# Pooling mixer rewritten as two TensorE products, and a new order of products in the FFN blocks

## The chip, the cores and the metric

The kernel runs on one core of a Trainium2 chip. The metric is the device time of one launch in microseconds (us). A core has TensorE (PE, with its weight loads listed apart as PEld), VectorE (DVE), ScalarE (ACT), GpSimd (POOL) and SyncE (SP); SP and POOL issue the transfers between the chip's memory and the on-chip memory.

## What is computed

Two layers over 512 tokens of 1024 channels, all float32. Each is: half a SwiGLU feed-forward step (FFN), a mixer, another half FFN step; layer 0's mixer pools, layer 1's convolves. The part that changes most is the pooling mixer:

```python
def pool_mixer(x, w_pool, b_pool, scale):
    # for each group g of 256 channels, window w in (2, 4, 8, 16):
    #   pooled[t] = mean of x[t - w/2 : t + w/2], cut at both ends, minus x[t]
    y = jnp.einsum('bsgc,gcd->bsgd', pooled, w_pool).reshape(B, S, D) + b_pool
    return y * scale
x = x + pool_mixer(rmsnorm(x, norm_g[0, 1]), pool_w[0], pool_b[0], pool_scale[0])
```

A norm's per-token factor r, and the pooling over tokens, commute with the product over channels, so each may be taken on either side of it.

## The kernel before, in words

The residual stream `x` lies on chip as 8 chunks of 128 channels x 512 tokens. Weights arrive as a list of numbered pieces (`pieces`, line 104), up to 128 x 1024, in the order in which they are used. A piece lands in one of 8 `raw` buffers, ACT rounds it to `whi` (line 178), DVE takes the remainder `wlo` (line 185), and a product is three matmuls, hi x hi, hi x lo, lo x hi (`passes`, line 199; lines 200 to 202). `whi` and `wlo` have 4 buffers each. `Norm.add` (line 214) makes the same pair `xh`, `xl` of a chunk of x and its square `sq`, which POOL adds up; `sums` reduces over channels with short matmuls and gives r; `spread` broadcasts r.

An FFN (`ffn`, line 332) has "heads" (4 PSUM banks, one 12-matmul group for each of the 8 chunks), then two phases of blocks (2 and 3 of them), each followed by the output product `ps_o` of 8 chunks in two parts (288 matmuls in phase 2). A block is seven products of 24 matmuls of 512 columns, of Strassen's kind, in the order of `STEPS` (line 39): b11, t1, b21, t2, t3, b22, t4, each with two weight pieces (called first and second piece below). Pieces of t1, t2, t4 are sums: POOL issues a transfer that adds a second matrix onto the raw buffer of an earlier piece of the chain b11, t1, t2, t4, as soon as that one has been converted (lines 168, 189). The s-operands (`sxh`, `sxl`) are sums of quarters of x, made by `Norm.pair` (line 241). A block's hidden values are transposed on PE (`ps_t`) and turned into `hh`, `hl` (lines 348, 350) during the next block, or within the output product behind the last block.

`pool_mixer` (line 479): 48 matmuls give the group product `ps_z`, channels on partitions. Then, chunk after chunk: DVE multiplies by r (line 500), ACT and POOL subtract the identity part from x (lines 503, 504), DVE and POOL form window sums by shifted additions or a running sum (lines 517 to 532), and DVE scales the edges and adds into x (lines 539 to 542); then the next norm's `add`. The heads of the next FFN wait for those chunks.

The order on each engine comes from a scheduler that simulates the program ahead of time; within a manual region the order written is kept.

Of the kernel before, what the change touches and what calls it, by code (L numbers as in the profile page):

```python
# [15 lines left out]
P = 128  # L16
# [8 lines left out]
WINDOWS = (2, 4, 8, 16)  # L25
HEAD = 6
# [12 lines left out]
STEPS = ("b11", "t1", "b21", "t2", "t3", "b22", "t4")  # L39
# [3 lines left out]
EDGE = 8  # L43
# [11 lines left out]
SPLIT_SUMS = ("g02",)  # L55
# [5 lines left out]
    ("dw", NC * KW), ("edge", len(WINDOWS) * 2 * EDGE),  # L61
# [10 lines left out]
def encoder(ctx: ExitStack, tc: tile.TileContext, xT, winh, win, wout, poolw, pw1, pw2h, pw2, vecs, out):  # L72
# [15 lines left out]
    for pool in (const, dpool):  # L88
        nc.vector.memset(pool.tile([P, 16], F32, name="pad"), 0.0)
    npbs = const.tile([P, NC], F32, name="npbs")  # L90
    pscw = const.tile([P, NC], F32, name="pscw")
# [25 lines left out]
    in_chunks = {(l, i): paired if (l, i) == (1, 0) else list(range(NC)) for l in range(2) for i in range(2)}  # L117
# [214 lines left out]
    def ffn(l, i, norm, nxt, pre=None):  # L332
# [19 lines left out]
        def gated_heads():  # L352
            for j in range(FH):
# [9 lines left out]
                two(j, u)  # L363

# [42 lines left out]
        def block(b, todo, first):  # L407
# [5 lines left out]
            product("b11", b, "a11", A, True, False, norm.spread if first else None)  # L413
# [65 lines left out]
    def pool_mixer(norm, nxt):  # L479
        pss = []  # L480
        with tc.manual_schedule(engines={mybir.EngineType.PE}):
            for c in range(NC):
                g, h = divmod(c, 2)
                if c % 4 == 0:
                    wh, wl = piece(("pw", g // 2))
                ps = psum.tile([P, S], F32, tag="mm", name="ps_z")
                for k in range(2):
                    o = ((g % 2) * 2 + k) * 256 + h * P
                    passes(ps, wh[:, o:o + P], wl[:, o:o + P], norm.hi[2 * g + k], norm.lo[2 * g + k], k == 0, k == 1)
                pss.append(ps)  # L490
                if c == 2:
                    norm.sums()
                if c == 4:
                    norm.spread()
        zs, wins = [], []

        def evacuate(c):
            if c < NC:
                zs.append(hpool.tile([P, S], F32, tag="h", name="z"))
                nc.vector.tensor_tensor(out=zs[c], in0=pss[c], in1=norm.rb, op=ALU.mult)  # L500

                u = hpool.tile([P, S], F32, tag="h", name="u")
                nc.scalar.activation(u, zs[c], AF.Identity, scale=vec("psc", c), bias=npbs[:, c:c + 1])
                nc.gpsimd.tensor_tensor(out=x[c], in0=x[c], in1=u, op=ALU.subtract)

        def window(c):

            if c >= NC:
                return
            w = WINDOWS[c // 2]  # L510
            b = w // 2
            z = zs[c]
            win = hpool.tile([P, S], F32, tag="h", name="win")
            wins.append(win)
            add = nc.vector if c in ADD_ON_VECTOR else nc.gpsimd
            if w == 2:
                add.tensor_copy(out=win[:, 0:1], in_=z[:, 0:1])
                add.tensor_tensor(out=win[:, 1:], in0=z[:, 1:], in1=z[:, :S - 1], op=ALU.add)
            elif w == 4:
                two = wpool.tile([P, D], F32, tag="raw", name="two", bufs=RAWS)  # L520
                add.tensor_copy(out=two[:, 0:1], in_=z[:, 0:1])
                add.tensor_copy(out=two[:, S:S + 1], in_=z[:, S - 1:S])
                add.tensor_tensor(out=two[:, 1:S], in0=z[:, 1:], in1=z[:, :S - 1], op=ALU.add)
                add.tensor_copy(out=win[:, 0:1], in_=two[:, 1:2])
                add.tensor_tensor(out=win[:, 1:], in0=two[:, 2:S + 1], in1=two[:, :S - 1], op=ALU.add)
            else:

                run = wpool.tile([P, D], F32, tag="raw", name="run", bufs=RAWS)
                nc.gpsimd.memset(run[:, 0:b + 1], 0.0)
                nc.vector.tensor_tensor_scan(out=run[:, b + 1:b + 1 + S], data0=ones_c.to_broadcast([P, S]), data1=z, initial=0.0, op0=ALU.mult, op1=ALU.add)  # L530
                nc.vector.tensor_copy(out=run[:, b + 1 + S:S + 2 * b], in_=run[:, b + S:b + S + 1].to_broadcast([P, b - 1]))
                nc.vector.tensor_tensor(out=win, in0=run[:, w:S + w], in1=run[:, :S], op=ALU.subtract)

        def mix(c):
            w = WINDOWS[c // 2]
            b = w // 2
            win = wins[c]
            e = vec("edge", (c // 2) * 2 * EDGE, 2 * EDGE)
            nc.vector.tensor_tensor(out=win[:, :b], in0=win[:, :b], in1=e[:, :b], op=ALU.mult)
# [497 lines left out]
```

## Time and profile before

| what | value |
|---|---|
| time, median of 3 runs | 1694.42 us (1693.49 to 1694.85) |
| the profiled execution | 1690.47 us, span 1688.6 us |
| PE busy | 1619.0 us, 96% of the span |
| granted TensorE clock, mean | 0.98 of full speed |
| moved | 241.62 MB, mean 143 GB/s |

In the profile a row gives an engine, the line of the kernel, the operation and `out<-in` by the program's names. Matmuls follow each other pipelined: their records overlap, so the distance of two starts is what one costs. The row `[2.75 <-ACT xh L223]` says that the engine stood idle for 2.75 us and what ended it.

### The profile page before, as it was taken

What the parts mean: (1) busy time and instruction counts of PE and PEld (TensorE: products, weight loads), DVE (VectorE), ACT (ScalarE), POOL (GpSimd) and SP (SyncE); (2) the same over time, 40 slices, a digit from 0 to 9 for tenths busy, and PEclk for the clock granted to TensorE, in tenths of its full rate; (3) what the DMA queues carried; (4) which work ended last, traced back from release to release, by engine and by line L of the source; (5) the groups of instructions that cost most, each with busy time, mean ns of one, the idle gap of its engine ahead of it and who ended that gap; (6) DMA issues with size and microseconds to landing.
All of it is one profiled execution on the core that took longest, in us unless ns stands there. A gap on an engine that the chain in (4) does not pass through costs nothing.

```text
span 1688.6 us, 19576 instructions
## 1 busy us (share of the span) xinstructions
PE 1619.0 (96%) x7244; PEld 1328.6 (79%) x7244; DVE 1105.2 (65%) x1411; ACT 786.3 (47%) x1138; POOL 379.5 (22%) x343
## 2 busy tenths in 40 slices
PE   8999999997899999999999999999999999999997
PEld 6788888875688887888788778887777888887785
DVE  8783677449875476665673667439987878367742
ACT  6442445334542344454432444478944645244431
POOL 5100110136110111012101110129982310011111
PEclk9999999998899999999999999999998999999998
DMA  8865886306583888327847886322102586588721
GB/s 255 198 147 151 194 208 167 93 20 162 144 171 117 195 193 186 124 84 176 195 118 170 192 199 162 114 64 66 47 10 75 151 199 144 150 191 206 169 63 50
DMA packets 75839, 241.62 MB, mean 143 GB/s; under 512 B 8544, under 2 KB 8672, under 8 KB 75744
## 3 DMA queue, kind: packets, MB, share of 16 engines
q1 hardware_dynamic: 52704, 156.48, 28.4%
q0 software_dynamic: 23040, 83.90, 28.1%
q8 instruction: 56, 0.92, 0.2%
q14 instruction: 39, 0.32, 0.1%
HBM read 238.25 MB, written 2.10 MB: 142 GB/s over the span
## 4 chain that ended last, share of the span: by engine, by line
PE 61%; DMA 14%; DVE 11%; issue 6%; ACT 5%; POOL 2%; POOLq 0%; DVEq 0%; ACTq 0%; SPq 0%
DMA raw<-win 14%; PE ps_o L202 9%; PE ps_o L200 9%; PE ps_o L201 9%; PE ps_a L200 4%; PE ps_a L202 4%; PE ps_a L201 4%; DVE wlo L185 4%; PE ps_c L201 3%; PE ps_c L200 3%; PE ps_c L202 3%; ACT whi L178 2%; PE ps_t L404 1%; ACT diag L612 1%; PE ps_b L201 1%
## 5 line engine op out<-in xcount | busy, mean ns | idle before, releaser
L185 DVE TENSOR_TENSOR wlo<-raw,whi 128x1024 fp32r<-128x1024 f32 (+2 forms) x468 | 521.0, 1117 | 429.1 <-ACT whi L178 424.1
L178 ACT CAST whi<-raw 128x1024 fp32r<-128x1024 f32 (+2 forms) x468 | 439.4, 944 | 700.6 <-DMA raw<-win 193.4
L168 POOL DMA_DIRECT2D raw<-win x160 | 141.4, 889 | 876.8 <-DMA raw<-win 405.3
L201 PE MATMUL ps_o<-hl,whi 128*128 128x512 f32 x704 | 273.6, 390 | 0.0
L202 PE MATMUL ps_o<-hh,wlo 128*128 128x512 f32 x704 | 273.5, 389 | 0.0
L200 PE MATMUL ps_o<-hh,whi 128*128 128x512 f32 x704 | 273.4, 390 | 0.0
L200 PE MATMUL ps_a<-whi,xh 128*128 128x512 f32 x480 | 189.2, 397 | 0.0
L202 PE MATMUL ps_a<-whi,xl 128*128 128x512 f32 x480 | 189.2, 395 | 0.0
L201 PE MATMUL ps_a<-wlo,xh 128*128 128x512 f32 x480 | 188.4, 393 | 0.0
L235 POOL TENSOR_TENSOR sq<-sq 128x512 f32<-128x512 f32 x47 | 76.1, 1619 | 355.1 <-ACT sq L230 354.6
L202 PEld LDWEIGHTS ps_o<-hh,wlo 128*128 128x128 f32 x704 | 132.2, 188 | 27.3
L201 PEld LDWEIGHTS ps_o<-hl,whi 128*128 128x128 f32 x704 | 132.2, 188 | 27.3
L200 PEld LDWEIGHTS ps_o<-hh,whi 128*128 128x128 f32 x704 | 132.1, 188 | 27.2
L200 PE MATMUL ps_c<-whi,sxh 128*128 128x512 f32 x320 | 125.8, 397 | 0.1
L201 PE MATMUL ps_c<-wlo,sxh 128*128 128x512 f32 x320 | 124.8, 390 | 0.5 <-DVE wlo L185 0.5
L202 PE MATMUL ps_c<-whi,sxl 128*128 128x512 f32 x320 | 124.8, 390 | 0.0
L642 POOL TENSOR_TENSOR part<-part,tap 128x509 f32<-128x509 f32 (+6 forms) x78 | 114.3, 1465 | 25.0 <-ACT tap L641 19.4
L200 PEld LDWEIGHTS ps_a<-whi,xh 128*128 128x128 f32 x480 | 91.7, 191 | 19.5
L202 PEld LDWEIGHTS ps_a<-whi,xl 128*128 128x128 f32 x480 | 90.8, 189 | 19.9
L201 PEld LDWEIGHTS ps_a<-wlo,xh 128*128 128x128 f32 x480 | 91.3, 190 | 19.0
L470 DVE SCALAR_TENSOR_TENSOR x<-ps_o,x 128x512 f32<-128x512 f32 x64 | 44.2, 691 | 63.7 <-PE ps_o L202 63.7
L201 PE MATMUL ps_b<-wlo,sxh 128*128 128x512 f32 x160 | 66.3, 414 | 10.2 <-DVE wlo L185 10.1
(174 smaller groups left out, 2591.2 us busy)
## 6 DMA issues: line engine op xcount, KB each, us to landing
raw<-win SPq DMA_DIRECT2D x160, 512.0 KB, 4.9
raw<-win POOLq DMA_DIRECT2D x160, 512.0 KB, 6.4
raw<-wout SPq DMA_DIRECT2D x64, 256.0 KB, 2.7
raw<-wout SPq DMA_DIRECT2D x32, 512.0 KB, 3.6
raw<-wout SPq DMA_DIRECT2D x32, 384.0 KB, 3.1
raw<-pw SPq DMA_DIRECT2D x18, 512.0 KB, 3.5
raw<-winh SPq DMA_DIRECT2D x32, 256.0 KB, 2.6
raw<-pw2h SPq DMA_DIRECT2D x8, 384.0 KB, 2.9
```

The lines of the kernel that those rows point to most:

```text
L168: nc.gpsimd.dma_start(out=t[:, :w], in_=more, accum_op=ALU.add)
L178: nc.scalar.copy(out=his[n][:, :w], in_=raws[n][:, :w])
L185: nc.vector.tensor_tensor(out=lo[:, :w], in0=raws[n][:, :w], in1=his[n][:, :w].bitcast(F32), op=ALU.subtract)
L200: nc.tensor.matmul(ps, whi, mhi, start=start, stop=False, skip_group_check=True)
L201: nc.tensor.matmul(ps, whi, mlo, start=False, stop=False, skip_group_check=True)
L202: nc.tensor.matmul(ps, wlo, mhi, start=False, stop=stop, skip_group_check=True)
L235: nc.gpsimd.tensor_tensor(out=self.acc, in0=self.acc, in1=sq, op=ALU.add)
L404: nc.tensor.transpose(ps[:, t * P:(t + 1) * P], ht[t][:, c * P:(c + 1) * P], ident)
L470: nc.vector.scalar_tensor_tensor(out=x[c], in0=pss[m], scalar=0.5, in1=x[c], op0=ALU.mult, op1=ALU.add)
L612: nc.scalar.activation(self.diags[-1][:, n % 2, q], ident, AF.Copy, scale=self.wtap[q][:, col:col + 1].bitcast(F32))
L642: nc.gpsimd.tensor_tensor(out=self.part[:, o], in0=self.part[:, o], in1=t[:, o], op=ALU.add)
```

## The change

1. The pooling mixer. The group product now has tokens on the output's partitions (x chunks stationary, 256 columns of the weights moving): 96 matmuls of 256 columns. ACT and DVE scale by r while they split the result into `zh` and `zl`. The pooling, the subtraction of the identity and the edges are a second product, with constant band matrices over tokens as moving operand (`window`): for each of 8 chunks one matmul of 512 columns, seven of 130 to 144, and for six chunks two more of 2 to 8 columns. Each DVE instruction then adds a chunk into x. `x += bias * scale` goes to ACT, ahead of it.
2. The bands: 8 transfers of 128 x 512 (256 KB) and 8 casts on ACT, called just ahead of the output product of phase 2 of FFN (0,0).
3. All blocks: the order of pieces is b11, b21, t1, t2, t3, b22, t4, and b11 and b21 finish one bank before the other is begun (`product_by_pair`).
4. FFN (0,1) takes its heads in the order 0, 4, 1, 5, ..., and the norm ahead of the mixer adds its last square on PE.

```diff
-STEPS = ("b11", "t1", "b21", "t2", "t3", "b22", "t4")
+STEPS = ("b11", "b21", "t1", "t2", "t3", "b22", "t4")
-SPLIT_SUMS = ("g02",)
+SPLIT_SUMS = ("g01", "g02")
...
+        def product_by_pair(step, b, quarter, banks, start, stop, between=None):
+            ws = [piece((step, l, i, b, 0)), piece((step, l, i, b, 1), AHEAD - 1)]
+            for p in range(2):
+                for k in range(KH):
+                    hi, lo = ws[k // 2]
+                    cs = slice((k % 2) * BW, (k % 2 + 1) * BW)
+                    passes(banks[p], *norm.quarter(quarter, k, p), hi[:, cs], lo[:, cs], start and k == 0, stop and k == KH - 1)
+                if p == 0 and between:
+                    between()
...
             A = pair_of_banks("ps_a")
-            product("b11", b, "a11", A, True, False, norm.spread if first else None)
+            product_by_pair("b11", b, "a11", A, True, False, norm.spread if first else None)
...
+            next_()
+            product_by_pair("b21", b, "a12", A, False, True)
+            m1 = [silu(A[p], p) for p in range(2)]
             B = pair_of_banks("ps_b")
             product("t1", b, "s1", B, True, True)
-            next_()
-            product("b21", b, "a12", A, False, True)
-            m1 = [silu(A[p], p) for p in range(2)]
...
+            if ph and last:
+                last()
             for n, (m, h) in enumerate(OUT_ORDER):
...
+    def load_bands():
+        tiles = []
+        for g in range(len(WINDOWS)):
+            two_ = []
+            for q in range(2):
+                raw = hpool.tile([P, S], F32, tag="h", name="band")
+                nc.sync.dma_start(out=raw, in_=bands[g, q])
+                two_.append(hpool.tile([P, S], F32R, tag="h", name="bandr"))
+                nc.scalar.copy(out=two_[q], in_=raw)
+            tiles.append(two_)
+        return tiles
...
+        def mixed(g):
+            gp, j = g % 2, g // 2
+            cs = slice(j * 256, j * 256 + 256)
+            for t in range(NT):
+                if j == 0:
+                    pz[gp][t] = psum.tile([P, S], F32, tag="mm", name="ps_z")
+                ts = slice(t * P, (t + 1) * P)
+                for k in range(2):
+                    wh, wl = w[g // 2]
+                    o = ((g % 2) * 2 + k) * 256
+                    c = 2 * g + k
+                    passes(pz[gp][t][:, cs], norm.hi[c][:, ts], norm.lo[c][:, ts], wh[:, o:o + 256], wl[:, o:o + 256], k == 0, k == 1)
+        def evacuate(gp):
+            for t in range(NT):
+                rt = norm.r[:, t:t + 1]
+                zh[gp][t] = hpool.tile([P, S], F32R, tag="h", name="zh")
+                nc.scalar.activation(zh[gp][t], pz[gp][t], AF.Copy, scale=rt)
+                zl[gp][t] = hpool.tile([P, S], F32R, tag="h", name="zl")
+                nc.vector.scalar_tensor_tensor(out=zl[gp][t], in0=pz[gp][t], scalar=rt, in1=zh[gp][t].bitcast(F32), op0=ALU.mult, op1=ALU.subtract)
+        def window(c):
...
+            for t in range(NT):
+                h_, l_ = zh[gp][t], zl[gp][t]
+                if t == 0:
+                    mm(slice(0, S), h_, first, True)
+                    mm(slice(0, P + e), l_, first[:, :P + e])
+                    if b > 1:
+                        mm(slice(0, b), h_, rest[:, BANDS[2]:BANDS[2] + b])
+                    continue
+                o = slice(t * P - e, min(S, (t + 1) * P + e))
+                at = BANDS[t == NT - 1]
+                m = rest[:, at:at + o.stop - o.start]
+                mm(o, h_, m)
+                if t == NT - 1 and b > 1:
+                    mm(slice(S - b, S), h_, rest[:, BANDS[3]:BANDS[3] + b])
+                mm(o, l_, m, False, t == NT - 1)
...
         with tc.manual_schedule(engines={mybir.EngineType.PE}):
+            w = [piece(("pw", 0)), piece(("pw", 1), AHEAD - 1)]
+            mixed(0)
+            norm.sums()
             for c in range(NC):
+                nc.scalar.activation(x[c], x[c], AF.Identity, bias=psb[:, c:c + 1])
+            mixed(2)
+            evacuate(0)
+            mixed(1)
+            for n, c in enumerate(in_chunks[0, 1]):
+                ps = window(c)
+                if n == 0:
+                    mixed(3)
+                    evacuate(1)
+                nc.vector.scalar_tensor_tensor(out=x[c], in0=ps, scalar=vec("psc", c), in1=x[c], op0=ALU.mult, op1=ALU.add)
+                nxt.add(c)
```

The order of instructions moves at three places that matter below. First PE in the pooling mixer, where the change puts the first chunk's window product between the third and the fourth of the four group products (`bandr` are the bands, `zh` and `zl` the split group product; the bank is `ps_w`):

```order
L202 MATMUL ps_z<-whi_2920,xl_2768 128x256
L540 MATMUL ps_w<-bandr,zh 128x512
L540 MATMUL ps_w<-bandr,zl 128x130
L540 MATMUL ps_w<-bandr,zh 128x132
L540 MATMUL ps_w<-bandr,zl 128x132
L540 MATMUL ps_w<-bandr,zh 128x130
L540 MATMUL ps_w<-bandr,zl 128x130
L200 MATMUL ps_z<-whi_2947,xh_2937 128x256
```

All eight window products and all of `ps_z` now stand ahead of the first head matmul; before, the heads followed `ps_z` directly and waited for DVE, ACT and POOL.

Second ACT in the output product of phase 2 of FFN (0,0). Before (`whi_2578` is the piece of the third chunk's second part, `whi_2608` that of the fourth chunk's first part):

```order
L178 CAST whi_2511<-raw_2509 128x512
L178 CAST whi_2578<-raw_2576 128x512
L348 CAST hh<-ps_t 128x512 x4
L178 CAST whi_2608<-raw_2606 128x1024
L178 CAST whi_2633<-raw_2631 128x512
```

Here the last block's four `hh` casts come directly behind the third chunk's second part. On the same engine at the same place with the change (`whi_2641` is now the fourth chunk's first part):

```order
L178 CAST whi_2544<-raw_2542 128x512
L502 CAST bandr<-band 128x512 x2
L178 CAST whi_2611<-raw_2609 128x512
L502 CAST bandr<-band 128x512 x3
L178 CAST whi_2641<-raw_2639 128x1024
L502 CAST bandr<-band 128x512 x3
L348 CAST hh<-ps_t 128x512 x4
L178 CAST whi_2666<-raw_2664 128x512
```

The four `hh` casts of the last block moved behind the fourth chunk's `whi` and behind the band casts.

Third PE in a block of phase 2 (`whi290` and `whi291` are t1's pieces before; with the change `whi292` and `whi293` are t1's, `whi290` and `whi291` b21's). Before, behind b11:

```order
L202 MATMUL ps_a_7606<-whi289_7555,xl3_5994 128x512
L200 MATMUL ps_b_7646<-whi290_7572,sxh_5701 128x512
L201 MATMUL ps_b_7646<-wlo290_7574,sxh_5701 128x512
...
L200 MATMUL ps_b_7646<-whi291_7607,sxh_5934 128x512
L200 MATMUL ps_b_7647<-whi291_7607,sxh_5934 128x512
...
L201 MATMUL ps_b_7646<-wlo291_7609,sxh_5934 128x512
...
L200 MATMUL ps_a_7605<-whi292_7626,xh4_5684 128x512
```

Here both pieces of t1 follow b11, and b21 comes behind them. With the change, on PE behind b11 of the same block:

```order
L202 MATMUL ps_a_7704<-whi289_7652,xl3_6091 128x512
...
L200 MATMUL ps_b_7790<-whi292_7748,sxh_5798 128x512
L200 MATMUL ps_b_7791<-whi292_7748,sxh_5798 128x512
...
L201 MATMUL ps_b_7790<-wlo292_7750,sxh_5798 128x512
...
L200 MATMUL ps_b_7790<-whi293_7753,sxh_6031 128x512
L200 MATMUL ps_b_7791<-whi293_7753,sxh_6031 128x512
L200 MATMUL ps_a_7703<-whi290_7671,xh4_5781 128x512
```

In this block, and in 11 others of the 20, t1's first piece still stands right behind b11, and b21 now stands between the first and the rest of the second piece; in the other eight, b21 goes ahead of nearly all of t1.

## Rows read from the trace of the kernel before

**Rows 1.** The page, part 1: busy time, share of the span, instructions

```profile
PE 1619.0 (96%) x7244; PEld 1328.6 (79%) x7244; DVE 1105.2 (65%) x1411; ACT 786.3 (47%) x1138; POOL 379.5 (22%) x343
```

**Rows 2.** Busy time of PE, PEld, DVE, ACT, POOL (count) by stretch; then clock, DMA share, GB/s

```profile
361.60:460.00 98.40, 75.66 (x301) 58.81 (x300) 82.31 (x118) 49.91 (x72) 40.30 (x39) 0.86 0.49 123
...
373.60:423.00 49.40, 34.19 (x127) 25.86 (x125) 45.90 (x62) 22.97 (x35) 32.20 (x32) 0.86 0.55 142
...
889.00:1010.00 121.00, 118.18 (x525) 96.60 (x524) 67.52 (x79) 45.60 (x54) 18.33 (x21) 1.00 0.79 187
```

**Rows 3.** Waits: us in total, times, longest; PE over the run, ACT from 330 to 450

```profile
PE ps_h L200 <- ACT xh L223: 11.1, 3, 7.9
PE ps_b L201 <- DVE wlo L185: 10.1, 13, 0.9
PE ps_b L200 <- ACT sxh L255: 6.7, 3, 3.5
...
ACT xh L223 <- DVE x L542: 15.6, 7, 3.8
```

**Rows 4.** PE in order of time, 361 to 451: start, duration, instruction, idle before

```profile
361.70 0.39 PE L200 MATMUL ps_z<-xh,whi 128*128 128x512 f32 x1
...
365.55 0.39 PE L202 MATMUL ps_z<-xh,wlo 128*128 128x512 f32 x1
...
377.37 0.73 PE L200 MATMUL ps_h<-xh,whi 128*128 128x512 f32 x2 [2.75 <-ACT xh L223]
...
382.06 0.63 PE L200 MATMUL ps_h<-xh,whi 128*128 128x512 f32 x1
382.48 0.61 PE L201 MATMUL ps_h<-xl,whi 128*128 128x512 f32 x1
...
397.10 2.07 PE L200 MATMUL ps_h<-xh,whi 128*128 128x512 f32 x4 [7.86 <-ACT xh L223]
...
429.45 0.50 PE L200 MATMUL ps_b<-whi,sxh 128*128 128x512 f32 x1 [3.53 <-ACT sxh L255]
...
450.30 0.61 PE L200 MATMUL ps_c<-whi,sxh 128*128 128x512 f32 x2
```

**Rows 5.** PE in order of time: the short matmuls in the mixer, and what follows

```profile
365.78 0.95 PE L288 MATMUL ps_sum<-ones_c,sq 128*128 128x1 f32 x8
...
366.58 0.49 PE L200 MATMUL ps_z<-xh,whi 128*128 128x512 f32 x1
...
369.45 1.05 PE L299 MATMUL ps_b<-ident,r 128*128 128x128 f32 x8
...
370.26 0.48 PE L200 MATMUL ps_z<-xh,whi 128*128 128x512 f32 x1
```

**Rows 6.** ACT and PE in order of time, output product of FFN (0,0), phase 2

```profile
306.14 2.06 ACT L348 CAST hh<-ps_t 128x512 fp32r<-128x512 f32 x4
312.75 1.05 ACT L178 CAST whi<-raw 128x1024 fp32r<-128x1024 f32 x1 [4.56 <-issue]
...
312.51 0.39 PE L202 MATMUL ps_o<-hh,wlo 128*128 128x512 f32 x1
```

**Rows 7.** POOL, ACT, PE in order of time, one block: t1's first piece, then t2's

```profile
953.03 0.88 POOL L168 DMA_DIRECT2D raw<-win  x1 [1.92 <-DVE wlo L185]
...
962.15 1.05 ACT L178 CAST whi<-raw 128x1024 fp32r<-128x1024 f32 x1 [8.07 <-DMA raw<-win]
...
964.51 0.50 PE L201 MATMUL ps_b<-wlo,sxh 128*128 128x512 f32 x1 [0.42 <-DVE wlo L185]
...
964.86 0.86 POOL L168 DMA_DIRECT2D raw<-win  x1 [7.32 <-DMA raw<-win]
...
970.55 1.06 ACT L178 CAST whi<-raw 128x1024 fp32r<-128x1024 f32 x1
```

**Rows 8.** PE in order of time: two waits in first blocks of other FFNs

```profile
44.38 0.50 PE L200 MATMUL ps_b<-whi,sxh 128*128 128x512 f32 x1 [2.69 <-ACT whi L178]
...
788.41 1.16 PE L299 MATMUL ps_b<-ident,r 128*128 128x128 f32 x8 [1.02 <-POOL r L294]
```

More of the change, by code (lines that the diff above doesn't have):

```diff
@@ L42 @@
 AHEAD = 4
-EDGE = 8
 RMS_EPS = 1e-6
@@ L60 @@
     ("pb", NC), ("psc", NC), ("ba", NC), ("bg", NC), ("bdw", NC), ("lng", NC), ("lnb", NC), ("b2", NC),
-    ("dw", NC * KW), ("edge", len(WINDOWS) * 2 * EDGE),
+    ("dw", NC * KW),
 )
@@ L71, in encoder @@
 @with_exitstack
-def encoder(ctx: ExitStack, tc: tile.TileContext, xT, winh, win, wout, poolw, pw1, pw2h, pw2, vecs, out):
+def encoder(ctx: ExitStack, tc: tile.TileContext, xT, winh, win, wout, poolw, bands, pw1, pw2h, pw2, vecs, out):
     nc = tc.nc
@@ L86, in encoder @@
     mhalf = const.tile([P, NT], F32, name="mhalf")
[L88 to L91, printed above, removed]
+    for pool, n in ((const, 88), (dpool, 16)):
+        nc.vector.memset(pool.tile([P, n], F32, name="pad"), 0.0)
+    psb = const.tile([P, NC], F32, name="psb")
     shift_w = const.tile([P, P], F32R, name="shift_w")
@@ L330, in head_tiles, with ffn @@
         return pss
-    def ffn(l, i, norm, nxt, pre=None):
+    def ffn(l, i, norm, nxt, pre=None, last=None):
         hh, hl = {}, {}
@@ new lines, in pool_mixer @@
+    def pool_mixer(norm, nxt, band):
+        gps = ((0, 2), (1, 3))
+        pz = [[None] * NT for _ in gps]
+        zh, zl = ([[None] * NT for _ in gps] for _ in range(2))
+        def mixed(g):
[18 more added lines that the diff above has]
+        def window(c):
+            g, h = divmod(c, 2)
+            gp, j = g % 2, g // 2
+            zs = slice(j * 256 + h * P, j * 256 + (h + 1) * P)
+            b = WINDOWS[g] // 2
+            e = max(b, 2)
+            first, rest = band[g]
+            ps = psum.tile([P, S], F32, tag="mm", name="ps_w")
+            mm = lambda o, z, m, start=False, stop=False: nc.tensor.matmul(ps[:, o], z[:, zs], m, start=start, stop=stop, skip_group_check=True)
+            for t in range(NT):
[13 more added lines that the diff above has]
+                mm(o, l_, m, False, t == NT - 1)
+            return ps
@@ L490, in pool_mixer @@
[L490 to L539, printed above, removed]
-            if b > 1:
-                nc.vector.tensor_tensor(out=win[:, S - b:], in0=win[:, S - b:], in1=e[:, 2 * EDGE - b:], op=ALU.mult)
-            nc.vector.scalar_tensor_tensor(out=x[c], in0=win, scalar=pscw[:, c:c + 1], in1=x[c], op0=ALU.mult, op1=ALU.add)
-            nxt.add_hi(c)
@@ L545, in pool_mixer @@
-        with ExitStack():
-            for c in range(2):
-                evacuate(c)
-                window(c)
-            for c in range(NC):
-                mix(c)
-                evacuate(c + 2)
-                window(c + 2)
-                nxt.add_lo(c)
+                nc.scalar.activation(x[c], x[c], AF.Identity, bias=psb[:, c:c + 1])
[9 more added lines that the diff above has]
+                nxt.add(c)
@@ L980, in encoder, with window_bands @@
         nc.sync.dma_start(out=out[c * P:(c + 1) * P, :], in_=o)
-def edge_factors():
-    e = np.ones((len(WINDOWS), 2 * EDGE), np.float32)
+def window_bands():
+    out = np.zeros((len(WINDOWS), 2, P, S), np.float32)
     for g, w in enumerate(WINDOWS):
         b = w // 2
-        for t in range(b):
-            e[g, t] = w / (t + b)
-            e[g, 2 * EDGE - b + t] = w / (w - t)
-    return np.broadcast_to(e.reshape(1, -1), (P, e.size))
+        e = max(b, 2)
+        t = np.arange(S)
+        lo, hi = np.clip(t - b, 0, S), np.clip(t + b, 0, S)
+        full = ((t[:, None] >= lo) & (t[:, None] < hi)) / (hi - lo) - np.eye(S)
+        short = np.ascontiguousarray(full.astype(np.float32))
+        short = (short.view(np.uint32) & np.uint32(0xFFFFE000)).view(np.float32)
+        rest = (full - short).astype(np.float32)
+        out[g, 0] = short[:P]
+        m = slice(P - e, 2 * P + e)
+        out[g, 1, :, BANDS[0]:BANDS[0] + P + 2 * e] = short[P:2 * P, m]
+        out[g, 1, :, BANDS[1]:BANDS[1] + P + e] = short[S - P:, S - P - e:]
+        out[g, 1, :, BANDS[2]:BANDS[2] + b] = rest[:P, :b]
+        out[g, 1, :, BANDS[3]:BANDS[3] + b] = rest[S - P:, S - b:]
+    return out
 def columns(v):
@@ L1011 @@
           "bdw": conv_b_dw, "lng": conv_ln_g, "lnb": conv_ln_b, "b2": conv_b_pw2}
-    cols = [columns(v[n]) for n, _ in VECS[:-2]]
+    cols = [columns(v[n]) for n, _ in VECS[:-1]]
     dw = np.asarray(conv_w_dw)[0].reshape(KW, NC, P).transpose(2, 1, 0).reshape(P, NC * KW)
```

24 lines of the change are left out of this document (8 added, 16 removed).

## The prediction

> **What bounds the kernel now.** I read the page first, then the stretches, then the waits, then the instructions in order of time. The page says that PE is busy 96% of the span [rows 1]; a table by stretch shows where the other 4% lies. In the blocks of FFN (1,0) PE is busy 118.2 of 121.0 us at full clock, but between 361.6 and 460 only 75.7 of 98.4 us, at a mean clock of 0.86 [rows 2]. That second stretch is the pooling mixer, the heads of FFN (0,1) and its first block. PE waits longest there for `xh` (11.1 us) and for `sxh` (6.7 us), and ACT, which makes `xh`, waited 15.6 us for DVE's last step on a chunk of x [rows 3]. So PE waits for the shifted additions on DVE and POOL; DVE is busy 45.9 of the 49.4 us from 373.6 to 423 [rows 2].
>
> A matmul of 512 columns costs 0.227 us: from 361.70 to 365.55 there are 17 steps [rows 4]. That is the 2.4 GHz level. Behind idle times the steps are 0.42 us (382.06 to 382.48, rows 4), the 1.2 GHz level.
>
> The stretch from the first `ps_z` (361.70) to the first matmul of t2 (450.30) takes 88.6 us [rows 4]. Its work at full clock is 48 matmuls of `ps_z`, 96 of the heads and 72 of b11, t1 and b21, 216 x 0.227 = 49.0 us, and some 40 short ones at 0.10 us: the eight of `ps_sum` take 0.80 us from 365.78 to 366.58, the eight of `ps_b` 0.81 us [rows 5]. So 53 us are work and 35 us are waits and low clock. This is what can be won.
>
> **The mixer's stretch with the change.** The same stretch ends at t2's first matmul, with the same three products done. Its PE work:
> - `ps_z`: 96 matmuls of 256 columns. The trace has none of this width. Half of 0.227 is the lower end (0.114), 0.227 the upper. I take 0.12, since records of 128 columns and of 1 column cost 0.10 alike [rows 5], so a weight load does not hold it above that: 11.5 us (10.9 to 21.8).
> - Windows: 8 matmuls of 512 columns (1.8 us), 12 of 2 to 8 columns at 0.10 (1.2 us), and 56 of 130 to 144 columns. For these the nearest row is `ps_b`, 128 columns: four products are written there as eight records, so a product costs 0.20 us and a record 0.10 [rows 5]. These bound the price from both sides; I take 0.21, a whole product with its columns scaled up, because nothing in the trace shows a short product in one record: 11.8 us (5.6 to 12.7). Together 14.8 us.
> - Heads 96 x 0.227 = 21.8, sums and broadcast 32 short ones 3.3, b11, t1 and b21 72 x 0.227 = 16.3.
>
> The sum is 67.7 us. What waits remain? The first window needs r and four evacuations. They run on ACT and DVE beside the two group products that follow the sums (5.8 us); an evacuation costs DVE what its average instruction costs in this stretch, 45.9 / 62 = 0.74 us [rows 2], four are 3 us and r about 2. The second four have three window products as cover. A chunk then needs one DVE add, `xh` and `xl`, some 1.5 us of DVE, against 1.9 us of its window on PE, and the heads begin only behind all windows, so `xh` is ready each time. The pairs for `sxh` have the heads, b11 and most of b21 as cover, over 30 us. If that cover failed, 6.7 us of `sxh` waits [rows 3] would be back. r of the next norm is asked for 12 matmuls into b11; the other FFNs show a wait of 1.0 us there [rows 8], which I add. So 68.7 in place of 88.6: **-19.9 us**, with ends at -9.6 (`ps_z` at 0.227) and -26 (windows at 0.10).
>
> **The bands.** Their 2 MB go where the transfers are not short, but their casts stand in ACT's order ahead of the `hh` casts of the last block. The `whi` between them cannot start before PE has finished the third chunk's first part, whose last matmul starts at 312.51 [rows 6]. Then ACT needs 1.05 us for it, three band casts and the first `hh` at 2.06 / 4 = 0.52 each [rows 6], so the first `hh` is there at 315.9. PE's next instruction needs just this `hh`; before, all four were done by 308.2. PE stands from 312.7 to 315.9, 3.2 us. Behind such an idle time (2.75 us at 377.37, rows 4) the step fell to 0.42; I allow seven such matmuls, 1.4 us. **+4.6 us** (0 to 6, 0 if the casts were not late).
>
> **The blocks.** PE's wait for `wlo` at t1 came 13 times, 10.1 us; a wait of 0.85 costs some 0.16 more, because records overlap, so 12.2 in all [rows 3]. The chain is in [rows 7]: POOL issues the sum at 953.03, it lands at 962.15 (9.1 us), ACT and DVE convert it, PE's second t1 matmul waits until 964.51. In 12 of 20 blocks the order keeps t1's first piece right behind b11, so this wait stays in part; the second piece gets b21 as cover. I take half: **-6 us** (-12 to 0). t2 now stands two pieces behind t1: its sum is issued at 964.86, has landed by 970.55 [rows 7], and is converted some 2.3 us later at 972.9 (1.06 for ACT, about as much again for DVE); t2 begins 48 matmuls and eight transposes (0.10 each) behind 964.51, at 976.2. So 3.3 us of slack. The first block of all waited 2.69 us for t1's piece [rows 8]; b21 now goes first: **-2.7 us**.
>
> The rest (vector constants, edge factors, POOL's squares) is work beside PE and counts nothing; its cover is PE's stream itself.
>
> **The sum.** -19.9 + 4.6 - 6.0 - 2.7 = -24.0 us. The profiled execution took 1690.47 us, 4 us below the median of the runs shown; from it 1666.5, from the median 1694.42 I predict **1670 us**. A change of 0.2% (3.4 us) is about what this kernel's measurement can tell from none.
>
> **The rivals.**
> - *Cheap short products.* If the 56 cost one record of 0.10, the windows take 8.6 us and the time is 1664. For it: the records of [rows 5]; against: each product there takes two. The Trainium skill, page "TensorE: Matmul & The Clock Gate", section "Back-to-back issue gap", says that a stream of weight load and matmul pairs has about 81 ns a matmul at 128 columns; an estimate by it puts the windows at 7.3 us and the time at some 1662. No row here shows a product of that width in one record; at 512 columns the page has 131 ns where the rows show 0.227 us, so there the two differ and the measurement stands.
> - *The blocks do not get what the change says.* Since t1's first piece stays behind b11 in 12 blocks, the wait may stay whole: 1676. For it the order; against, that the wait at the second piece must go.
> - *The wait moves to t2 and grows; slower.* t2's sum now has only its own first piece's time as slack, since b21 no longer stands between t1 and t2. With the 5.7 us of [rows 7] from issue to landing 3.3 us are left; so a landing of L makes each block wait L - 9.0. At 9.1, what t1's sum took [rows 7], it just fits. At 11 the wait is 2.0 us a block, 40 us over 20 blocks, and the time 1710. It decides from (24.0 + 3.4) / 20 = 1.4 us a block, a landing of 10.4. For it: the transfers are busy in the blocks (share 0.79, rows 2); against: the 5.7 measured for this very sum.
> - *Dear group products.* `ps_z` at 0.227: 1680.
>
> **How the numbers follow.** Forecast 0.50, whose own range is 1665 to 1674; cheap products 0.20; blocks without gain 0.16; dear products 0.05; t2 wait 0.06; the rest, a mix of these, 0.03. The range 1656 to 1686 takes in the cases from cheap products with the blocks' waits all gone (another 6 us) to dear products with 6 us more in the blocks, and leaves out the t2 case. Faster by over 0.2%: 0.50 + 0.20 + 0.16 + 0.05 and 0.01 of the rest, 0.92; slower: 0.05 of the t2 case's 0.06; same: what is left, 0.03.
>
> **What would show it.** Right: from the first `ps_z` to t2's first matmul some 69 us with clock near 1; no wait for `xh` of a head; an idle time of about 3.2 us on PE ended by ACT `hh` in the output product of FFN (0,0); window steps of 0.20 to 0.21; waits at t1 fewer than 13, none of note at t2. Wrong: waits of over 1 us at `ps_c` in most blocks; steps of 0.10 or of 0.227 at the windows; PE waiting for `zh`, `zl` or the bands.

## The result and the profile after

The changed kernel takes **1652.72 us** (median of 4 runs, 1650.85 to 1661.36), the kernel before on the same chip 1694.63 us. The ratio is 0.9758, 95% interval 0.9735 to 0.9781: 42 us faster, where I had predicted 24, and outside my range of 1656 to 1686. A second measurement of the same kernel gave 0.9783 (0.9763 to 0.9803).

The page of the changed kernel, part 1, the answer to [rows 1]: busy time, share of the span, instructions.

```profile
PE 1620.0 (98%) x7368; PEld 1339.2 (81%) x7368; DVE 1086.2 (65%) x1377; ACT 794.8 (48%) x1153; POOL 357.6 (22%) x320
```

PE is busy as long as before (1620.0 us for 1619.0) in a span that is 29.8 us shorter, 1658.8 for 1688.6. So on balance the gain is idle time; busy time moves too, but it rises in one place and falls in another (both are below). The 29.8 us are less than the 42 of the medians, because each profile shows a single execution: that of before took 4 us less than the median of its runs, that of the change 8.6 us more.

The waits of PE after, us in total, times, longest; to be held against [rows 3].

```profile
PE ps_b L200 <- ACT whi L178: 3.2, 2, 2.3
...
PE ps_o L200 <- ACT hh L348: 3.0, 1, 3.0
PE ps_b L299 <- POOL r L294: 2.5, 1, 2.5
...
PE ps_b L201 <- DVE wlo L185: 0.6, 3, 0.2
```

The waits for `xh` (11.1 us) and for `sxh` (6.7) are gone. The wait for `hh` that I had predicted is there. The last row I had predicted at half its size only: the waits for `wlo` at t1 went from 10.1 us in 13 to 0.6 us in 3.

By stretch, the answer to [rows 2]: busy time of PE, PEld, DVE, ACT, POOL (count), then clock, DMA share, GB/s. The first row goes from the first `ps_z` to the first matmul of t2, the second over the blocks of FFN (1,0), phase 2.

```profile
365.05:428.65 63.60, 63.60 (x381) 56.60 (x380) 48.06 (x73) 41.21 (x65) 17.01 (x15) 1.00 0.52 133
...
892.10:1011.30 119.20, 119.06 (x537) 97.48 (x537) 86.05 (x100) 56.64 (x66) 17.40 (x20) 1.00 0.80 193
```

The mixer's stretch takes 63.6 us in place of 88.6, PE is busy in all of it and the clock is 1.00. I had said 68.7. Inside it, PE in order of time from the last `ps_z` to the second chunk's window, and the first head matmul: start, duration, instruction.

```profile
379.10 0.28 PE L201 MATMUL ps_z<-wlo,xh 128*128 128x256 f32 x1
379.22 0.28 PE L202 MATMUL ps_z<-whi,xl 128*128 128x256 f32 x1
379.34 0.40 PE L540 MATMUL ps_w<-bandr,zh 128*128 128x512 f32 x1
379.57 0.22 PE L540 MATMUL ps_w<-bandr,zl 128*128 128x132 f32 x1
379.64 0.39 PE L540 MATMUL ps_w<-bandr,zh 128*128 128x4 f32 x2
379.86 0.27 PE L540 MATMUL ps_w<-bandr,zl 128*128 128x136 f32 x1
379.97 0.28 PE L540 MATMUL ps_w<-bandr,zh 128*128 128x136 f32 x1
...
387.71 0.44 PE L200 MATMUL ps_h<-xh,whi 128*128 128x512 f32 x1
```

A product of 256 columns steps by 0.12 us, as I took it. A window product of 130 to 144 columns steps by 0.11 (379.86 to 379.97), half of what I took. The row `x2` holds a product of 4 columns and, by the order in `window`, one of 136 behind it; the two take 0.22 us (379.64 to 379.86), so the narrow one costs about as much as the wide one. All windows take 9.3 us: the 68 products from 379.34 to 387.71 are 8.4, the first chunk's eight 0.96.

PE, then ACT, in order of time at the bands, the idle time before in brackets; then the stretch behind, as in the table above.

```profile
313.09 1.65 PE L200 MATMUL ps_o<-hh,whi 128*128 128x512 f32 x3 [3.00 <-ACT hh L348]
314.54 0.63 PE L201 MATMUL ps_o<-hl,whi 128*128 128x512 f32 x1
314.97 0.63 PE L202 MATMUL ps_o<-hh,wlo 128*128 128x512 f32 x1
```

```profile
309.96 1.04 ACT L178 CAST whi<-raw 128x1024 fp32r<-128x1024 f32 x1 [1.43 <-PE ps_o L201]
310.91 1.65 ACT L502 CAST bandr<-band 128x512 fp32r<-128x512 f32 x3
312.47 2.03 ACT L348 CAST hh<-ps_t 128x512 fp32r<-128x512 f32 x4
```

```profile
313.10:319.20 6.10, 6.10 (x14) 4.80 (x15) 2.46 (x4) 1.40 (x3) 0.00 (x0) 0.50 0.31 89
```

This is the chain of the prediction: the cast of a weight piece waits for PE, three band casts follow, then the first `hh`. PE stands 3.00 us (predicted 3.2). Behind it the steps are 0.43 us from 313.1 to 319.2, where the profile gives a granted clock of 0.50, the 1.2 GHz level (the third number from the end), and this costs more than I allowed: the product from its first `ps_o` (291.84) to the first `ps_z` takes 73.2 us against 67.1 before, 6.1 us more.

Now the blocks. First a row that [rows 7] does not have, from the same block of the kernel before: PE at t1's second piece.

```profile
967.62 0.71 PE L404 MATMUL ps_t<-ident,ht 128*128 128x128 f32 x5
...
969.18 0.50 PE L201 MATMUL ps_b<-wlo,sxh 128*128 128x512 f32 x1 [0.85 <-DVE wlo L185]
```

PE waited 0.42 us for the first piece's `wlo` (964.51), and 0.85 us for the second's. Of the 13 waits of that profile 10, with 8.2 of the 10.1 us, stand at the second piece.

POOL, ACT and PE in order of time in a block of FFN (1,0) with the change, which answers to [rows 7]. POOL issues the sums of t1's first and second piece and of t2's first; ACT casts these three; PE's rows are t1's first matmuls, the first use of its second piece's `wlo`, and t2's first.

```profile
924.99 0.87 POOL L168 DMA_DIRECT2D raw<-win  x1 [1.95 <-DVE wlo L185]
928.64 0.87 POOL L168 DMA_DIRECT2D raw<-win  x1 [2.78 <-DVE wlo L185]
937.27 0.86 POOL L168 DMA_DIRECT2D raw<-win  x1 [7.76 <-DVE wlo L185]
```

```profile
934.56 1.05 ACT L178 CAST whi<-raw 128x1024 fp32r<-128x1024 f32 x1 [2.45 <-PE ps_a L202]
936.74 1.05 ACT L178 CAST whi<-raw 128x1024 fp32r<-128x1024 f32 x1 [0.52 <-DMA raw<-win]
942.90 1.05 ACT L178 CAST whi<-raw 128x1024 fp32r<-128x1024 f32 x1 [4.14 <-DMA raw<-win]
```

```profile
935.68 0.49 PE L415 MATMUL ps_t<-ident,ht 128*128 128x128 f32 x3
935.92 0.71 PE L200 MATMUL ps_b<-whi,sxh 128*128 128x512 f32 x2
936.47 0.49 PE L415 MATMUL ps_t<-ident,ht 128*128 128x128 f32 x3
936.92 0.50 PE L201 MATMUL ps_b<-wlo,sxh 128*128 128x512 f32 x1
...
945.35 0.39 PE L201 MATMUL ps_b<-wlo,sxh 128*128 128x512 f32 x1
...
947.66 0.48 PE L200 MATMUL ps_c<-whi,sxh 128*128 128x512 f32 x1
```

From the issue of the first sum to PE's first use of `wlo` it is 11.9 us here and 11.5 before: the first piece has hardly more time. Six transposes and a second `whi` matmul now stand there, and in this block no wait is recorded. The second piece gets the time: from the issue of its sum to the first use of its `wlo` it is 16.7 us here (928.64 to 945.35, behind the whole of b21), where the kernel before issued it at 956.68 and asked for it within 11.7 us, at 968.3. And t2's sum, issued at 937.27, is cast at 942.90, 5.6 us later; t2 begins at 947.66 without a wait. So the rival that ended slower did not happen.

### The profile page after: what moved, and what is told of

The parts are those of the page before. It is cut to its first block, busy times and chain, and to the rows that moved or that the text cites. A ratio compares the mean times of both kernels' runs of the same rounds, so it can differ in the third digit from the quotient of the medians.

```text
span 1658.8 us, 19786 instructions
## 1 busy us (share of the span) xinstructions
PE 1620.0 (98%) x7368; PEld 1339.2 (81%) x7368; DVE 1086.2 (65%) x1377; ACT 794.8 (48%) x1153; POOL 357.6 (22%) x320
## 4 chain that ended last, share of the span: by engine, by line
PE 78%; DVE 6%; DMA 6%; ACT 5%; issue 3%; POOL 1%; SPq 0%; DVEq 0%; POOLq 0%; ACTq 0%
PE ps_o L200 10%; PE ps_o L201 10%; PE ps_o L202 10%; PE ps_a L200 7%; PE ps_a L202 7%; PE ps_a L201 7%; DMA raw<-win 6%; PE ps_c L200 4%; PE ps_c L201 4%; PE ps_c L202 4%; PE ps_b L201 2%; DVE wlo L185 2%; PE ps_b L202 2%; PE ps_t L415 2%; PE ps_b L200 2%
## 5 line engine op out<-in xcount | busy, mean ns | idle before, releaser
L202 PEld LDWEIGHTS ps_c<-whi,sxl 128*128 128x128 f32 x320 | 60.1, 188 | 12.9
```

What stands on the lines that cost most here:

```text
L202: nc.tensor.matmul(ps, wlo, mhi, start=False, stop=stop, skip_group_check=True)
```

## Experiments

What each kernel's profile shows by stretch, in us: the **mixer** from the first `ps_z` to t2's first matmul in FFN (0,1); the **product** from the first `ps_o` of FFN (0,0), phase 2, to `ps_z`; the **blocks**, all 20 (first `ps_a` of a phase to its first `ps_o`, in FFN (0,1) from t2's first matmul); the **conv** mixer from its first `ps_mm` to its next `ps_h`. The ratio is to the kernel before, on the same chip.

| kernel | mixer | product | blocks | conv | span | ratio, interval |
|---|---|---|---|---|---|---|
| before | 88.6 | 67.1 | 803.9 | 164.8 | 1688.6 | |
| before again | 86.5 | 67.1 | 810.2 | 168.2 | 1695.9 | 0.9997 (0.9973, 1.0020) |
| change | 63.6 | 73.2 | 788.8 | 168.4 | 1658.8 | 0.9758 (0.9735, 0.9781) |
| change again | 63.6 | 73.3 | 788.7 | 167.1 | 1656.7 | 0.9783 (0.9763, 0.9803) |
| mixer alone | 64.9 | 72.0 | 810.1 | 166.6 | 1678.3 | 0.9900 (0.9882, 0.9918) |
| blocks alone | 84.8 | 67.1 | 783.5 | 168.8 | 1667.5 | 0.9878 (0.9858, 0.9897) |
| old order, by pair | 64.1 | 72.0 | 810.7 | 164.8 | 1675.7 | 0.9904 (0.9886, 0.9923) |
| new order, by piece | 63.6 | 72.0 | 785.1 | 164.7 | 1649.2 | 0.9742 (0.9721, 0.9763) |
| the same again | 63.6 | 72.0 | 788.9 | 166.8 | 1655.5 | 0.9753 (0.9727, 0.9779) |
| late bands | 63.6 | 67.1 | 785.7 | 167.1 | 1648.2 | 0.9763 (0.9736, 0.9789) |
| the same again | 63.6 | 67.0 | 790.0 | 167.1 | 1651.6 | 0.9750 (0.9723, 0.9776) |
| late bands, by piece | 63.6 | 67.0 | 790.2 | 168.4 | 1654.0 | 0.9735 (0.9709, 0.9761) |
| band casts on POOL | 63.6 | 69.5 | 790.3 | 169.2 | 1658.0 | 0.9769 (0.9741, 0.9797) |
| short products three times | 68.9 | 71.9 | 786.8 | 167.2 | 1658.5 | 0.9797 (0.9776, 0.9817) |

Mixer and product repeat to 0.1 us where nothing was edited that touches them. Blocks and conv scatter by 7 and 4.5 us from one execution to the next, so a single profile doesn't give their worth.

**The change again** (nothing edited).

> The change once more, nothing edited. What is open: its profiled execution took 1661.36 us, 8.6 us above the median of its runs (1652.72), at a mean clock of 0.985 where the other runs show 0.989. In that profile the conv stretch (first ps_mm to first ps_h behind it) is 168.4 us against 164.8 in the profile of before, and the end (first ps_sum of the last norm to the end) 18.2 against 17.2. Theory A: the 8.6 us are that one execution's own half-clock stretches in conv and at the end, not of the change; a new profile shows conv within 165 and the other stretches as before within 0.5 us, median 1650 to 1654. Theory B: the change itself makes conv slower by 3.6 us and some other stretch of the profile faster in the other runs; then conv is again at 168.

Measured 1656.22 us, conv 167.1. Theory A's stretches for mixer and product hold, its conv of 165 and its median of at most 1654 do not. Nor does theory B's blame on the change: conv shows 164.7 to 164.8 in three of the fourteen profiles, one of them with the new order of the pieces, and 166.6 to 169.2 in the others, the second profile of before among them. Neither theory is right as it was put.

**One part at a time.** The mixer alone takes back the order and the products of the blocks:

```diff
-STEPS = ("b11", "b21", "t1", "t2", "t3", "b22", "t4")
+STEPS = ("b11", "t1", "b21", "t2", "t3", "b22", "t4")
-            product_by_pair("b11", b, "a11", A, True, False, norm.spread if first else None)
+            product("b11", b, "a11", A, True, False, norm.spread if first else None)
...
-            next_()
-            product_by_pair("b21", b, "a12", A, False, True)
-            m1 = [silu(A[p], p) for p in range(2)]
             B = pair_of_banks("ps_b")
             product("t1", b, "s1", B, True, True)
+            next_()
+            product("b21", b, "a12", A, False, True)
+            m1 = [silu(A[p], p) for p in range(2)]
```

> The changed mixer, bands and mixer norm, with the old order and products of the blocks. Theory A (the parts add, each worth what its stretch shows): -25.1 us from first ps_z to first t2 matmul, less what b21 ahead of t1 gave in that stretch (about 1 us), and +6.2 at the bands: some -18 us, 1676 to 1677; the thirteen or so waits for wlo at t1 (10 us) are there again. Theory B (the waits at t1 were late because the mixer delayed the queues, not for the order of the steps): the waits are gone here too and the time is about 1662. Theory C (my prediction's own: sum for these parts -19.9 + 4.6): 1679.

The blocks alone do the opposite to the kernel before: the new order and `product_by_pair`, the old mixer.

> The old mixer with the new order of the steps and the products of b11 and b21 by pair. Theory A: the waits for wlo at t1 go (from 10.1 us to under 1), nothing new at t2, sum of the stretches of the blocks -15.4 us: 1679. Prediction's own terms: -6.0 - 2.7 = -8.7, 1686. Rival: part of the 15.4 comes from the mixer's change (lighter POOL, other load of the queues): 1683 to 1686 and some waits at t1 stay. The mixer's stretch itself is as before within 2 us (88.6).

Measured 1675.43 for the mixer alone (-17.8 us on its chip's 1693.23) and 1672.09 for the blocks alone (-21.1); the sum, -38.9, is within 2 us of the change's own -37.0 there. So the parts add. For the mixer theory A was right. For the blocks it was too small: it had compared two profiles, one of them the fortunate one. (The blocks alone also shorten the mixer's stretch, by 2 to 4 us, since an FFN's first block lies in it.) The waits for `wlo` in the mixer alone and in the blocks alone:

```profile
PE ps_b L201 <- DVE wlo L185: 11.4, 17, 0.9
```

```profile
PE ps_b L201 <- DVE wlo L185: 2.2, 5, 1.3
```

In the blocks alone 1.3 of the 2.2 us are one wait in the first block behind the old mixer.

**Which edit of the blocks does it.** First the change with the old order of the steps, b11 and b21 still by pair:

```diff
-STEPS = ("b11", "b21", "t1", "t2", "t3", "b22", "t4")
+STEPS = ("b11", "t1", "b21", "t2", "t3", "b22", "t4")
...
-            next_()
-            product_by_pair("b21", b, "a12", A, False, True)
-            m1 = [silu(A[p], p) for p in range(2)]
             B = pair_of_banks("ps_b")
             product("t1", b, "s1", B, True, True)
+            next_()
+            product_by_pair("b21", b, "a12", A, False, True)
+            m1 = [silu(A[p], p) for p in range(2)]
```

> The change with the old order of the steps (t1 ahead of b21), b11 and b21 still by pair. Theory A (the order of the pieces alone gives the sum for t1 its time): the waits for wlo at t1 are back, 13 to 17 of them, 10 to 11 us, the blocks' stretches are as with the mixer alone, and the time is 16 to 20 us over the change, 1672 to 1676. Rival B (by pair both pieces of b11 are converted early, so that the sum starts early, and that is what took the waits away): no waits at t1, time within 3 us of the change, 1654 to 1659.

Then the new order with b11 and b21 piece by piece (`product` in place of `product_by_pair` in both calls):

> The change with b11 and b21 piece by piece, in the new order of the steps. Theory A: the waits at t1 stay away and the time is that of the change within 3 us, 1653 to 1659; the first block of an FFN may wait some 0.5 to 1 us more for r at the broadcast, since its place in b11 moves. Rival B: some 10 us of waits for wlo at t1 are back, 1668 to 1672.

Measured 1678.0 us, 2 over theory A's range, and 1650.01 (1653.45 in its repetition), 3 under it. The waits of PE, in the kernel with the old order:

```profile
PE ps_b L201 <- DVE wlo L185: 13.9, 19, 0.9
```

With the new order by piece that row is absent from the whole list; what is left at t1 are waits for `whi`, all at the first piece:

```profile
PE ps_b L200 <- ACT whi L178: 3.7, 3, 1.9
```

So it is the order of the pieces that takes the waits away, and not `product_by_pair`. The ratios by piece (0.9742, 0.9753) and by pair (0.9758, 0.9783) overlap: whether going by pair costs anything these runs can't tell; it gains nothing they can show.

**The kernel before again.** For the size of the blocks' gain.

> The kernel before once more, nothing edited. What is open: the blocks' stretches (first ps_a of each group of blocks to its first ps_o, in FFN (0,1) from the first t2 matmul) sum to 803.9 us in its first profile, but to 810.1 and 810.7 in the two kernels with the old order of the steps, and conv takes 164.8 where most others show 166.6 to 169.2; that profile also lay 4 us under the median of its runs. Theory A (that profile was a fortunate one; the old order costs the blocks 20 to 25 us against the new one, 784 to 790): blocks 806 to 812, conv 165 to 169, time 1692 to 1698, wlo waits at t1 13 to 19. Theory B (the blocks of the kernel before are faster than those of the mixer alone, so part of the gain is taken back in kernels with the new mixer): blocks at 804 within 1 us.

Theory A holds: 1692.84 us, blocks 810.2, conv 168.2, 17 waits. Its eight stretches of blocks have this sum of busy times (span summed, then PE, PEld, DVE, ACT, POOL):

```profile
30.70:119.10 88.40, 84.08 (x369) 68.47 (x368) 69.62 (x86) 44.06 (x55) 15.34 (x17) 0.96 0.79 180
...
783.90:869.50 85.60, 82.09 (x362) 66.57 (x362) 61.54 (x75) 39.57 (x48) 12.63 (x13) 0.98 0.73 167
...
sum 810.20, PE 788.17 PEld 642.09 DVE 587.23 ACT 376.70 POOL 118.25; mean PE 98.52 PEld 80.26 DVE 73.40 ACT 47.09 POOL 14.78
```

The same eight in the change again:

```profile
758.40:838.20 79.80, 79.60 (x362) 65.59 (x362) 60.38 (x74) 37.73 (x47) 12.47 (x13) 1.00 0.77 179
...
sum 788.50, PE 780.76 PEld 641.04 DVE 584.84 ACT 375.19 POOL 117.87; mean PE 97.59 PEld 80.13 DVE 73.10 ACT 46.90 POOL 14.73
```

Before, PE is idle for 810.2 - 788.2 = 22.0 us of them, after for 7.7: 14.3 us of the gain. The other 7.4 us are busy time with the same matmuls; around a wait the records no longer overlap, and the clock is lower in stretches with long waits (0.96 and 0.98 in the two rows shown). How the 7.4 us divide between the two was not worked out.

Where the idle time went, by PE's waits in the same two profiles, before again, then change again:

```profile
PE ps_b L201 <- DVE wlo L185: 12.2, 17, 0.9
...
PE ps_b L299 <- POOL r L294: 4.6, 3, 2.3
...
PE ps_b L200 <- ACT whi L178: 3.4, 3, 2.4
```

```profile
PE ps_b L200 <- ACT whi L178: 4.6, 4, 1.7
...
PE ps_b L201 <- DVE wlo L185: 1.0, 5, 0.2
PE ps_b L299 <- POOL r L294: 1.0, 1, 1.0
```

Read one by one, 11 of the 17 waits for `wlo` (8.7 of 12.2 us) stand at t1's second piece, and none of the five after. At the first piece the waits stay: for `wlo` and `whi` together 4.6 us before and 5.6 after, and over all profiles 2.7 to 6.5 us in the four with the old order, 2.9 to 6.1 in the ten with the new one. The second row is another gain of the order that neither theory named: r. In the phase-1 blocks of FFN (1,0), the second of the stretches shown, DVE makes `v`, from which POOL makes r, behind the `wlo` of a piece that came late; with the new order `v` comes as soon as the sums are there. DVE in order of time, before again, then change again:

```profile
787.16 1.22 DVE L185 TENSOR_TENSOR wlo<-raw,whi 128x1024 fp32r<-128x1024 f32 x1 [7.21 <-ACT whi L178]
788.31 0.15 DVE L292 TENSOR_SCALAR v<-ps_sum 128x4 f32<-128x4 f32 x1
```

```profile
758.59 0.16 DVE L292 TENSOR_SCALAR v<-ps_sum 128x4 f32<-128x4 f32 x1 [1.42 <-PE ps_sum L288]
```

**The price of a short product.** Window products of the low part done three times:

```diff
-                mm(o, l_, m, False, t == NT - 1)
+                for n in range(3):
+                    mm(o, l_, m, False, n == 2 and t == NT - 1)
```

> The change with each of the 32 window products of the low part (130 to 144 columns) done three times: 64 more short products, and so the low part of the group products counted three times in the pooled result. Theory A (a short product costs one record of about 0.11 us): the stretch of ps_w is longer by 64 x 0.11 = 7.0 us and the time 7 us over the change. Rival B (a short product costs two records, 0.21 us, as the prediction took it): 13.4 us over the change.

The edit reaches only the three later token blocks of each chunk, since the first has a line of its own; so 24 products are tripled, not 32, and 48 are added, not 64. Theory A then asks 5.3 us, B 10.1. The mixer's stretch grew from 63.6 to 68.9, 5.3 us, 0.110 each. PE in order of time there:

```profile
377.81 0.50 PE L540 MATMUL ps_w<-bandr,zl 128*128 128x136 f32 x3
378.15 0.27 PE L540 MATMUL ps_w<-bandr,zh 128*128 128x136 f32 x1
378.26 0.50 PE L540 MATMUL ps_w<-bandr,zl 128*128 128x136 f32 x3
```

Three products with the same operands start within 0.34 us and the single one behind them within 0.11. Theory A holds. The time, 1660.06 us, lies 3.8 and 7.3 us over the change's two medians, which by itself would not tell 5.3 from 10.1 well.

**The bands.** They are loaded and cast six output pieces later:

```diff
-            if ph and last:
-                last()
...
+                if ph and last and n == FIRST + 3:
+                    last()
                 out_part(ph, m, h, pss[m])
```

> The change with the bands loaded and cast six output pieces later, behind the hh casts of the last block. Theory A: PE's idle time of 3.0 us ended by ACT hh at the output product of FFN (0,0) goes, and with it the half clock behind it: the stretch from its first ps_o to ps_z is 67.1 instead of 73.3, and the time 6 us less than the change: 1646 to 1647. Rival B: the casts are now in the way of whi or xh in that product or the first windows wait for bands, and the gain is under 2 us. Rival C: the 6.2 us are not of the casts (hh late for whi's wait alone): the idle time is still 1.5 us and the gain 3.

And, with their place kept, cast on POOL (`nc.gpsimd.tensor_copy` for `nc.scalar.copy`), so that only the weight piece's cast still stands ahead of `hh` on ACT:

> The change with the casts of the bands on POOL in place of ACT; ACT's order is otherwise that of the change, with one cast of a weight piece (whi100, which waits for PE's end of the third chunk's first part) ahead of the hh casts. Theory A: PE's idle time at the output product of FFN (0,0) is what stays of ACT's work behind that PE end, 1.05 + 0.5 = 1.6 us, in place of 3.0, and the half clock behind it is shorter or none; stretch ps_o to ps_z 69 to 70 us against 73.3 in the change and 67.0 with the bands late: time 1652 to 1654. Rival: the 6.2 us need the casts on ACT alone, the idle time goes wholly and the stretch is 67: 1650 to 1652. Against both: POOL's casts are so slow that the first window waits for bands, then the wait stands at ps_w.

With POOL casting, PE's wait at that product:

```profile
312.34 0.98 PE L200 MATMUL ps_o<-hh,whi 128*128 128x512 f32 x3 [1.44 <-ACT hh L348]
```

and with the late bands no wait is left in the whole product:

```profile
291.90:358.90 67.00, 67.00 (x305) 55.72 (x304) 30.89 (x40) 33.91 (x51) 8.95 (x6) 1.00 0.39 116
```

Both stretches came as theory A had them, 67.1 and 69.5. So of the change's 6.2 us about half is the idle time and half the low clock behind it; without the band casts 1.4 us of idle time stays, for the one weight piece. The times were less kind: 1651.87 for the late bands beside the change's 1656.22 (-4.4, expected -6), 1655.76 with POOL (expected 1652 to 1654), and the intervals of all three ratios overlap.

**A version of both.** Late bands with b11 and b21 by piece, beside the two that it is made of.

> Candidate: the change with the bands late and b11, b21 piece by piece, the new order of the steps kept. Theory A (the two edits add): no idle time at hh in the output product of FFN (0,0), stretch from its ps_o to ps_z 67, blocks with no waits for wlo at t1; 4 to 5 us under the products by piece alone, so 1645 to 1648, and 0 to 4 us under the bands late with products by pair. Rival B (by piece and by pair are the same, what they differed by lies in conv's half-clock stretches, 164.7 in one profile against 167.1 in the other): the same as the late bands by pair within 2 us.

> The late bands with products by pair once more, beside the other two on one chip, nothing edited: 1648 to 1652, stretch from ps_o of FFN (0,0) to ps_z 67.1.

> The products by piece with the bands where the change has them, once more: 1649 to 1653; if it is 4 us over the late bands by piece, the bands' place is worth that in both forms of the products.

Measured 1651.37, 1653.12 and 1653.45 us: 2.1 us apart at most, so the time came as rival B had it and not 4 to 5 us apart as theory A did, where the bands' 5 us are plainly in the product's stretch (67.0, 67.0 and 72.0). In these profiles the blocks (790.2 and 790.0 against 788.9) and conv (168.4 and 167.1 against 166.8) were longer, both within their scatter. The lowest ratio of the study, 0.9735, is this version's; it beats the kernel before by 2.6%, and the change by an amount that the intervals don't separate from none.

## Why the prediction was wrong

The direction and the places were right; several terms were mis-sized, the blocks' and the windows' most of all.

- **The blocks: "I take half: -6 us".** This is the largest error. Measured: 810 to 811 us with the old order in three of four profiles, 783.5 to 790.3 in all ten with the new one, some 21 us, against 6.0 + 2.7. The mechanism was right as argued: t1's first piece, still right behind b11 in 12 blocks, keeps its waits (2.7 to 6.5 us with the old order, 2.9 to 6.1 with the new), and the second piece gets b21 as cover and loses all of its own. The half was the wrong step. I had read one wait in order of time, at the first piece [rows 7], and split 12.2 us evenly; but 10 of the 13 waits, 8.2 of 10.1 us, stood at the second piece in that same trace, so the argument itself asked for some 10 us in place of 6. Transposes don't explain it: five of them stood ahead of the second piece's `wlo` before, and PE still waited 0.85 us (969.18). Besides, I had counted the waits in one profile, 13 with 10.1 us; the other three of that order show 17 to 19 and 11.4 to 13.9 us. I had not counted at all that r comes earlier at the first blocks of other FFNs (3.3 us of idle time in the blocks of the two second profiles), nor that PE's busy time falls with the waits, by 7.4 us there, of which the 0.16 a wait that I had allowed is 2.7 for 17 waits.
- **The first block of all: "-2.7 us".** The wait for t1's piece went, but a wait for r came in the same block: 2.5 to 2.6 us in seven of the ten profiles with the new order, 1.0 in three. So little of this term was won.
- **The windows: "I take 0.21".** Measured 0.11 (0.110 each in the tripled products), 9.3 us for the windows in place of 14.8. I had chosen the nearest row by width, `ps_b` at 128 columns, where four products leave eight records [rows 5]. But those operands, r and the identity, are plain float32 in the code, while zh, zl and the bands are float32r, as the operands of `ps_z` are. Its 48 products leave 48 records in the kernel before, 16 for each of the three lines:

```profile
L200 PE MATMUL ps_z<-xh,whi x16: 389/389/486, 361.7 to 373.8; 128*128 128x512 f32 x16
```

The row to choose was one with the same type; by it, one record each, the windows' term was that of the rival of cheap products. That the type makes the difference is read from these rows and was not tried by itself. Nor was it so that "nothing in the trace shows a short product in one record": the transposes, of 128 columns, leave 320 records for 320 of them, and I had priced them at 0.10 myself. The Trainium skill, page "TensorE: Matmul & The Clock Gate", section "Back-to-back issue gap", has about 81 ns for 128 columns, so it pointed the right way; the rows show 110 ns at 130 to 144 columns, and the measurement stands.
- **"r ... 1.0 us, which I add".** It did not come in this stretch: PE is busy in all 63.6 us of it. With the new mixer and the old order it did come, 1.02 us at 425.19 in the mixer alone; so the order of the pieces took it away, here as in FFN (1,0). The windows' 5.5 us and this one would make 62.2 of my 68.7; the other terms came out 1.4 us longer, most of it at the short matmuls.
- **The bands: "+4.6 us".** The idle time was right, 3.00 for 3.2. The low clock behind it lasted some 14 matmuls where I allowed seven, and the term is +6.1 in the change's two profiles; in the five other kernels with the same idle time of 3.00 us it is some +4.9, near what I had put.
- **Right as put:** `ps_z` at 0.12; no wait for `xh`, `sxh`, `zh`, `zl` or the bands; t2 without a wait, with a landing of 5.6 us (5.7 predicted).

The sum again, with what was measured, by the two second profiles (before again, change again): mixer 86.5 to 63.6, -22.9; product +6.2; blocks -21.5; conv -1.1; together -39.3, and the spans differ by 39.2.

Both second profiles lie above the medians of their runs, by 5.0 and 3.0 us. The range failed at its lower end: 1656 was cheap products and another 6 us of waits, that is the blocks' gain at 12 + 2.7, where their stretches gave some 21.

## What to carry to other kernels

Price an operation by the row with the same operand type before the row with the same width. Before a row of waits is shared out between consumers that a change treats differently, list where each of them stands: here one row held two consumers, and the one that the change covers had four fifths of it. And a wait that recurs in every block should be counted in several executions (13 and 17 times in two of the same kernel); its cost is the idle time and also the busy time that it stretches, and what stands behind it in order on another engine, here `v` for r, is late with it.

## What was not expected of the hardware

In these rows a float32r product with a new stationary operand steps by 0.11 us from 4 up to 144 columns, by 0.12 at 256 and by 0.227 at 512: below 256 columns the width is nearly free. Behind an idle time of 3.00 us the 1.2 GHz level (granted clock 0.50) lasted until 319.2, 6.1 us, and the stretch lost 3.1 us beyond the idle time; in five other kernels with the same 3.00 us it lost some 1.9. Behind 1.44 us (band casts on POOL) the granted clock stayed at 1.00 from 312.3 to 316, and the stretch lost 1.0 us beyond the idle time, 0.4 of it a wait for `hl`. Why the blocks and conv of one and the same kernel differ by 6 and 3 us between executions stays open; no run here was made for it.
